# Two kernels fused at a double norm: one closed-form factor from both token sums in place of two factors taken in sequence

## The chip, the cores and the metric

The program runs on one core of one Trainium2 chip, in a single launch. The metric is the device time of the launch in microseconds (us), as the median of several executions. A second execution is taken with the hardware profiler; its records are the trace that is read here.

## The reference

Two transformer blocks run one behind the other on the same 256 tokens of width 1024, all in float32. Each block has two layers, each layer is feed-forward, mixer, feed-forward, and each of these begins with an RMS norm. The place of the change is the seam between the blocks, where two norms follow each other with nothing in between but the gains:

```python
EPS = 1e-6

def rmsnorm(x, g):
    xf = x.astype(jnp.float32)
    y = xf * lax.rsqrt(jnp.mean(xf * xf, axis=-1, keepdims=True) + EPS)
    return (y * g.astype(jnp.float32)).astype(x.dtype)
...
    return rmsnorm(x, final_norm)          # end of the first block
...
        h = modulate(rmsnorm_2(x, norm_g[l, 0]), mod[:, 0], mod[:, 1])   # start of the second, l = 0
        x = x + 0.5 * mod[:, 2][:, None, :] * swiglu_2(h, ffn_w1[l, 0], ffn_w2[l, 0])
```

With s1 the sum of x² over a token and s2 the sum of (g·x)², g being `final_norm`, the first factor is r1 = (s1/1024 + EPS)^-½, and the second norm sees the values r1·g·x, whose squares add up to r1²·s2. Its factor is r2 = (r1²·s2/1024 + EPS)^-½. The second block's feed-forward needs the product r1·r2 for its input, and r1 alone for the residual x.

## The kernel before

The activations are kept transposed: `x` is a tile of 128 partitions × 8 blocks × 256 tokens, the width being 8 × 128. Each matmul is made in fp32r parts: a value v is split in a rounded high part and the low rest, so that a weight chunk becomes `wh` (made on ACT at line 311) and `wl` (made on DVE at line 324, `wl = stg - wh`, in two halves of 128×1024), and the norm input becomes `Hh` and `Hl`. Weights stream from memory in chunks of 16 blocks through the staging tiles `stg`; the class `Stream` decides which chunk is prepared when. A scheduler puts the instructions of each engine in order when the program is built; each engine then runs its own list in order, with semaphores between engines.

A feed-forward (`ffn`, line 724) computes 22 output tiles; tile i takes 16 weight blocks. The norm's factor is not applied to its input. The first five tiles (`i < OLD`) multiply the gained but unnormed x (lines 614 to 616, three matmuls per block, `pp` in PSUM) and get the token's factor afterwards, as `t = pp * rs` on DVE at line 742, where `rs` holds the factor of each token in all 128 partitions. Meanwhile `renorm` (line 570) makes the normed input `H` block by block, which the tiles from the fifth on read (lines 598 and 599, two matmuls per block).

So the factor is made beside the first tiles, in three steps that sit in the middle of tile 1. After block 1 `norm_sum` runs. `token_sums` (line 518) has PE add up the squares over the partitions, two matmuls of one column each into a PSUM tile `pst`; `inv_root` (line 525) has DVE make the mean plus EPS (`ms`, line 529) and POOL raise it to the power -½ (`rcol`, line 531). After block 7 `norm_spread` has PE copy the factor of each token to all partitions (line 537, two transposes into `pbc`), and ACT copies that to `rs` (line 562).

All norms but one are single. The one at the seam, announced by `turn` (line 715) with `fin` set to the gain `final_norm`, has two accumulators of squares, `acc` and `acc2`, and takes two factors in sequence (lines 543 to 551). It spreads two of them: `rcol` is the product of both factors, for the feed-forward, and `r1` is the first one, by which `renorm` rescales x (line 588). In this text the stretch from the token sums to the spread is called the seam. Before it, on DVE, stand two products of the background work on the modulation (line 693), and after it the first `t`.

The helper tiles of the norm (`ms`, `rcol`, `q`, `q2`, `rc2`, `rs`) come from the pool `tp`, one place per tag and buffer. The pools of each stage (`act`, `H`, the mixers' tiles) are opened later and lie behind it in the on-chip memory.

Of the kernel before, what the change touches and what calls it, by code (L numbers as in the profile page):

```python
# [9 lines left out]
F32 = mybir.dt.float32  # L10
# [3 lines left out]
OP = mybir.AluOpType  # L14
# [3 lines left out]
P = 128  # L18
S = 256
D = 1024  # L20
# [5 lines left out]
EPS = 1e-6  # L26
# [344 lines left out]
class Kern:  # L371
# [166 lines left out]

    def norm_sum(self):
        nc, tp = self.nc, self.tp  # L540
        self.rcol = self.inv_root(self.token_sums(self.acc), D)
        if self.fin is not None:
            r1 = self.rcol
            q = tp.tile([P, 2], F32, name="q", tag="q")
            nc.vector.tensor_mul(q, r1[:, :2], r1[:, :2])
            q2 = tp.tile([P, 2], F32, name="q2", tag="q2")
            nc.vector.tensor_mul(q2, self.token_sums(self.acc2), q)
            r2 = self.inv_root(q2, D)
            self.rcol = tp.tile([P, 8], F32, name="rc2", tag="rc2")
            nc.vector.tensor_mul(self.rcol[:, :2], r1[:, :2], r2[:, :2])  # L550
            self.r1 = r1

    def norm_spread(self):
        self.rs = self.spread_rows(self.rcol)
# [1137 lines left out]
```

## Time and profile before

| | |
|---|---|
| median of 3 runs | 1996.35 us (1993.39 to 1996.38) |
| the profiled execution, its own time | 1991.56 us |
| span of its trace | 1989.8 us |
| PE busy | 1956.1 us (98%) |
| DVE busy | 1588.7 us (80%) |
| ACT busy | 1176.2 us (59%) |
| POOL busy | 188.9 us (9%) |
| granted TensorE clock, mean | 0.997 of full speed |

The span runs from the first to the last instruction that the profiler saw; 1.76 us of the execution's time lie around it. PE is TensorE's matmuls, DVE is VectorE, ACT is ScalarE and POOL is GpSimd. Matmuls are pipelined and their ends are modelled, so that the step from one matmul to the next is read from their starts. The seam lies at about 1011 to 1018 us of the span.

### The profile page before, as it was taken

Reading aid. Unit: us, or ns where it says so; the run is one execution under the profiler, and the core shown is the slowest. Engines: PE = TensorE matmul, PEld = TensorE weight load, DVE = VectorE, ACT = ScalarE, POOL = GpSimd, SP = SyncE. Lnnn points to the kernel's source line nnn. Section 1 sums busy time; section 2 is a strip of 40 time slices with the busy share of each in tenths; the row PEclk is TensorE's granted clock in tenths of the full one; section 3 lists DMA queues with packets and bytes.
Section 4 is the critical chain, followed back from the end, with each engine's and each line's share of the span. In section 5 each row is a group of like instructions: output and inputs, shape, how many; then the busy total and the mean of one; then the engine's idle time right before and its main releaser. Section 6 shows DMA issues by size and latency. Waiting matters only on the chain.

```text
span 1989.8 us, 33083 instructions
## 1 busy us (share of the span) xinstructions
PE 1956.1 (98%) x13146; PEld 1776.8 (89%) x13146; DVE 1588.7 (80%) x2572; ACT 1176.2 (59%) x1977; POOL 188.9 (9%) x207
## 2 busy tenths in 40 slices
PE   8999999999999999999999999999999999999998
PEld 8888989888988898988898889898899888889887
DVE  8986788987888788898789878898667666988663
ACT  6654566554555466655566546675546554877652
POOL 3001012000100101200110010120010001211001
PEclk9999999999999999999999999999999999999999
DMA  7976435887687643488758864368555556315551
GB/s 290 334 279 242 161 137 176 296 288 268 231 290 273 244 153 143 171 299 290 266 193 304 290 239 166 128 246 290 183 195 179 190 191 199 128 50 194 189 186 61
DMA packets 67868, 429.36 MB, mean 216 GB/s; under 512 B 11392, under 2 KB 14208, under 8 KB 16896
## 3 DMA queue, kind: packets, MB, share of 16 engines
q1 hardware_dynamic: 66992, 426.19, 59.6%
q8 instruction: 103, 1.69, 0.3%
q10 hardware_dynamic: 720, 1.05, 0.2%
q14 instruction: 53, 0.43, 0.1%
HBM read 426.16 MB, written 1.05 MB: 215 GB/s over the span
## 4 chain that ended last, share of the span: by engine, by line
PE 87%; DVE 8%; ACT 2%; issue 1%; DMA 1%; POOL 0%; SPq 0%; POOLq 0%; ACTq 0%; DVEq 0%
PE pp L598 25%; PE pd L598 16%; PE pp L599 13%; PE pd L599 8%; PE pp L614 5%; PE pp L615 5%; PE pp L616 5%; PE po L889 3%; DVE wl L324 3%; PE pt L1279 1%; ACT wh L311 0%; PE pav L1574 0%; POOL rcol L531 0%; PE pd L782 0%; DVE e L1068 0%
## 5 line engine op out<-in xcount | busy, mean ns | idle before, releaser
L324 DVE TENSOR_TENSOR wl<-stg,wh 128x1024 fp32r<-128x1024 f32 x642 | 779.7, 1241 | 122.0 <-PE pd L599 46.2
L311 ACT ACTIVATE wh<-stg 128x1024 fp32r<-128x1024 f32 x642 | 662.6, 1053 | 318.1 <-PE pp L598 106.8
L598 PE MATMUL pp<-H,wh 128*128 128x512 f32 x2176 | 754.8, 390 | 0.0
L599 PE MATMUL pp<-H,wl 128*128 128x256 f32 x2176 | 613.7, 282 | 0.0
L598 PEld LDWEIGHTS pp<-H,wh 128*128 128x128 f32 x2176 | 408.4, 188 | 85.1
L598 PE MATMUL pd<-act,wh 128*128 128x512 f32 x1386 | 480.8, 390 | 0.0
L599 PEld LDWEIGHTS pp<-H,wl 128*128 128x128 f32 x2176 | 412.1, 189 | 0.0
L599 PE MATMUL pd<-act,wl 128*128 128x256 f32 x1386 | 390.9, 282 | 0.0
L614 PE MATMUL pp<-Hh,wh 128*128 128x256 f32 (+1 forms) x1176 | 338.9, 288 | 6.8 <-ACT wh L282 6.4
L616 PE MATMUL pp<-Hh,wl 128*128 128x256 f32 (+1 forms) x1176 | 332.9, 283 | 0.6 <-DVE wl L324 0.6
L615 PE MATMUL pp<-Hl,wh 128*128 128x256 f32 x1176 | 332.7, 283 | 0.6 <-DVE Hl L679 0.6
L598 PEld LDWEIGHTS pd<-act,wh 128*128 128x128 f32 x1386 | 260.1, 188 | 54.4
L599 PEld LDWEIGHTS pd<-act,wl 128*128 128x128 f32 x1386 | 262.6, 189 | 0.0
L614 PEld LDWEIGHTS pp<-Hh,wh 128*128 128x128 f32 x1176 | 222.8, 189 | 10.8 <-ACT wh L282 6.4
L615 PEld LDWEIGHTS pp<-Hl,wh 128*128 128x128 f32 x1176 | 224.1, 191 | 1.7 <-DVE Hl L679 1.2
L616 PEld LDWEIGHTS pp<-Hh,wl 128*128 128x128 f32 x1176 | 223.6, 190 | 1.4 <-DVE wl L324 0.8
L693 DVE SCALAR_TENSOR_TENSOR stg<-stg,cond 128x1024 f32<-128x1024 f32 x144 | 176.3, 1226 | 29.2 <-DMA stg<-mw 27.0
L675 ACT ACTIVATE act<-a 128x256 fp32r<-128x256 f32 x176 | 73.4, 417 | 140.4 <-DVE a L751 127.8
L515 POOL TENSOR_TENSOR acc<-sq 128x256 f32<-128x256 f32 x16 | 17.8, 1116 | 1169.8 <-ACT sq L511 1169.7
L515 POOL TENSOR_TENSOR acc<-acc,sq 128x256 f32<-128x256 f32 x87 | 78.4, 904 | 337.7 <-ACT sq L511 336.8
L676 DVE TENSOR_TENSOR act<-a,act 128x256 fp32r<-128x256 f32 x176 | 75.3, 428 | 44.0 <-ACT act L675 44.0
L738 ACT ACTIVATE s<-t 128x256 f32<-128x256 f32 x136 | 56.6, 416 | 77.1 <-DVE t L607 76.9
(318 smaller groups left out, 2134.0 us busy)
## 6 DMA issues: line engine op xcount, KB each, us to landing
stg<-b SPq DMA_DIRECT2D x132, 1024.0 KB, 4.8
stg<-a SPq DMA_DIRECT2D x129, 1024.0 KB, 4.8
stg<-mw SPq DMA_DIRECT2D x72, 1024.0 KB, 5.4
stg<-m SPq DMA_DIRECT2D x32, 1024.0 KB, 4.8
stg<-m2a SPq DMA_DIRECT2D x14, 1024.0 KB, 4.9
stg<-m2b SPq DMA_DIRECT2D x12, 1024.0 KB, 4.7
stg<-nab SPq DMA_DIRECT2D x4, 1024.0 KB, 4.7
cond<-cond SPq DMA_DIRECT2D x6, 512.0 KB, 4.9
```

The lines of the kernel that those rows point to most:

```text
L311: self.k.nc.scalar.activation(h[:, sl], self.raw[c][:, sl], AF.Copy)
L324: self.k.nc.vector.tensor_sub(l[:, sl], t[:, sl], f(h[:, sl]))
L515: nc.gpsimd.tensor_tensor(s2, acc, sq, op=OP.add)
L598: mm(p, h, parts, start=start, stop=False)
L599: return mm(p[:, :S], l, parts[:, 1], start=False, stop=stop)
L614: mm(out[:, :n], h, self.Hh[:, kt, :n], start=start and clear, stop=False, skip_group_check=not clear)
L615: mm(out[:, :S], h, self.Hl[:, kt], start=False, stop=False, skip_group_check=not clear)
L616: return mm(out[:, :n], l, self.Hh[:, kt, :n], start=False, stop=stop, skip_group_check=not clear)
L675: nc.scalar.activation(hi, src, AF.Copy)
L676: nc.vector.tensor_sub(lo, src, f(hi))
L693: self.nc.vector.scalar_tensor_tensor(sl, sl, 1.0, self.cond, op0=OP.mult, op1=OP.mult, accum_out=self.mod[l][:, 2 * c + g:2 * c + g + 1])
L889: mm(p, w, x[:, kt], start=half + kt + n + i // 4 == 0, stop=half == 1 and kt == 3 and n == 2, skip_group_check=True)
```

## The change

The double norm no longer takes the second factor from the first one. Since r1² = 1/m with m = s1/1024 + EPS, the product of both factors has a closed form, r1·r2 = (s2/1024 + EPS·m)^-½. Both sums are taken first; DVE makes m (`ms`), s2/1024 (`q`) and EPS·m + q (`q2`), and POOL takes two powers that don't depend on each other, first that of `q2` (the product, `rcol`) and then that of `ms` (the first factor, `r1`). Three multiplications and one mean on DVE go, two other small operations come, and the tile `rc2` is gone.

```diff
     def norm_sum(self):
         nc, tp = self.nc, self.tp
-        self.rcol = self.inv_root(self.token_sums(self.acc), D)
-        if self.fin is not None:
-            r1 = self.rcol
-            q = tp.tile([P, 2], F32, name="q", tag="q")
-            nc.vector.tensor_mul(q, r1[:, :2], r1[:, :2])
-            q2 = tp.tile([P, 2], F32, name="q2", tag="q2")
-            nc.vector.tensor_mul(q2, self.token_sums(self.acc2), q)
-            r2 = self.inv_root(q2, D)
-            self.rcol = tp.tile([P, 8], F32, name="rc2", tag="rc2")
-            nc.vector.tensor_mul(self.rcol[:, :2], r1[:, :2], r2[:, :2])
-            self.r1 = r1
+        if self.fin is None:
+            self.rcol = self.inv_root(self.token_sums(self.acc), D)
+            return
+
+        p, p2 = self.token_sums(self.acc), self.token_sums(self.acc2)
+        m = tp.tile([P, 8], F32, name="ms", tag="ms")
+        nc.vector.tensor_scalar(m[:, :2], p, 1.0 / D, EPS, op0=OP.mult, op1=OP.add)
+        q = tp.tile([P, 2], F32, name="q", tag="q")
+        nc.vector.tensor_scalar(q, p2, 1.0 / D, None, op0=OP.mult)
+        q2 = tp.tile([P, 2], F32, name="q2", tag="q2")
+        nc.vector.scalar_tensor_tensor(q2, m[:, :2], EPS, q, op0=OP.mult, op1=OP.add)
+        self.rcol, self.r1 = [tp.tile([P, 8], F32, name="rcol", tag="rcol", bufs=4) for _ in range(2)]
+        for r, w in ((self.rcol, q2), (self.r1, m[:, :2])):
+            nc.gpsimd.tensor_tensor(r[:, :2], w, self.mhalf[:, :2], op=OP.pow)
```

The scheduler also orders the engines' lists anew around it. On DVE, in the kernel before, the seam runs from the first mean to the first `t`, with the two halves of one weight chunk's `wl` between:

```order
L529 TENSOR_SCALAR ms_10521<-pst_10518 128x2
L324 TENSOR_TENSOR wl_10631<-stg_10335,wh_10506 128x1024
L545 TENSOR_TENSOR q_10525<-rcol_10523 128x2
L324 TENSOR_TENSOR wl_10631<-stg_10335,wh_10506 128x1024
L547 TENSOR_TENSOR q2_10527<-pst_10528,q_10525 128x2
L529 TENSOR_SCALAR ms_10532<-q2_10527 128x2
L550 TENSOR_TENSOR rc2_10536<-rcol_10523,rcol_10534 128x2
L742 TENSOR_TENSOR t_10566<-pp_10452,rs_10559 128x512
```

In the changed kernel the same place on DVE reads:

```order
L547 TENSOR_SCALAR ms_10524<-pst_10518 128x2
L549 TENSOR_SCALAR q_10526<-pst_10521 128x2
L324 TENSOR_TENSOR wl_10627<-stg_10335,wh_10506 128x1024
L551 SCALAR_TENSOR_TENSOR q2_10528<-ms_10524,q_10526 128x2
L324 TENSOR_TENSOR wl_10627<-stg_10335,wh_10506 128x1024
L745 TENSOR_TENSOR t_10562<-pp_10452,rs_10555 128x512
```

None of the small operations waits for POOL any more, but `q2`, the input of the first power, stands behind the first half of `wl` and ahead of the second.

On PE, in the kernel before, the spread stands within a triple of matmuls of tile 1 (`pp_10503`), 28 matmuls behind the token sums:

```order
L616 MATMUL pp_10503<-Hh_72,wl_10393 128x258
L614 MATMUL pp_10503<-Hh_72,wh_10337 128x258
L537 MATMUL pbc_10556<-ident_75,rc2_10536 128x128 x2
L537 MATMUL pbc_10561<-ident_75,rcol_10523 128x128 x2
L615 MATMUL pp_10503<-Hl_73,wh_10337 128x256
```

In the changed kernel it stands 18 matmuls behind the sums:

```order
L619 MATMUL pp_10503<-Hh_72,wl_10393 128x258
L537 MATMUL pbc_10552<-ident_75,rcol_10530 128x128 x2
L537 MATMUL pbc_10557<-ident_75,rcol_10531 128x128 x2
L617 MATMUL pp_10503<-Hh_72,wh_10337 128x258
L618 MATMUL pp_10503<-Hl_73,wh_10337 128x256
```

The four transposes moved ten matmuls ahead, and both pairs still stand side by side; the second pair now reads the result of POOL's second power (`rcol_10531`).

Behind the seam DVE's list is reordered in places up to the end of this feed-forward. In the kernel before, the rows from the first `a` on are:

```order
L753 SCALAR_TENSOR_TENSOR a_10572<-t_10566,b_10568,s_10570 128x256
L742 TENSOR_TENSOR t_10619<-pp_10503,rs_10559 128x512
L685 TENSOR_REDUCE b_10621<-pp_10503 128x2
L324 TENSOR_TENSOR wl_10636<-stg_10388,wh_10628 128x1024
L676 TENSOR_TENSOR act_10451<-a_10572,act_10451 128x256
```

In the changed kernel:

```order
L756 SCALAR_TENSOR_TENSOR a_10568<-t_10562,b_10564,s_10566 128x256
L591 SCALAR_TENSOR_TENSOR x_70<-x_70,cols_74,rs_10560 128x256 x2
L580 TENSOR_TENSOR y_10669<-x_70,rs_10555 128x256
L679 TENSOR_TENSOR act_10451<-a_10568,act_10451 128x256
L679 TENSOR_TENSOR H_10572<-h_10575,H_10572 128x256
L679 TENSOR_TENSOR H_10572<-h_10593,H_10572 128x256
L745 TENSOR_TENSOR t_10615<-pp_10503,rs_10555 128x512
L688 TENSOR_REDUCE b_10617<-pp_10503 128x2
L324 TENSOR_TENSOR wl_10632<-stg_10388,wh_10624 128x1024
```

Two rescalings of x, one `y`, the first `act` and two parts of `H` moved ahead of the second `t` and of the next `wl`.

## Rows read from the trace of the kernel before

**Rows 1.** The page: busy time by engine, and the chain that ended last.
```profile
PE 1956.1 (98%) x13146; PEld 1776.8 (89%) x13146; DVE 1588.7 (80%) x2572; ACT 1176.2 (59%) x1977; POOL 188.9 (9%) x207
...
PE 87%; DVE 8%; ACT 2%; issue 1%; DMA 1%; POOL 0%; SPq 0%; POOLq 0%; ACTq 0%; DVEq 0%
```

**Rows 2.** PE's waits, 1010 to 1040 us: us in total, times, longest.
```profile
PE pbc L537 <- DVE rc L550: 1.7, 1, 1.7
```

**Rows 3.** Timeline at the seam, DVE and POOL: start us, length us.
```profile
1011.68 1.22 DVE L693 SCALAR_TENSOR_TENSOR stg<-stg,cond 128x1024 f32<-128x1024 f32 x1
...
1012.83 0.15 DVE L529 TENSOR_SCALAR ms<-pst 128x2 f32<-128x2 f32 x1
1012.90 1.21 DVE L324 TENSOR_TENSOR wl<-stg,wh 128x1024 fp32r<-128x1024 f32 x1
...
1013.06 1.62 POOL L531 TENSOR_TENSOR rcol<-ms,mhalf 128x2 f32<-128x2 f32 x1 [3.50 <-DVE ms L529]
...
1014.71 0.16 DVE L545 TENSOR_TENSOR q<-rcol 128x2 f32<-128x2 f32 x1 [0.60 <-POOL rcol L531]
...
1014.79 1.22 DVE L324 TENSOR_TENSOR wl<-stg,wh 128x1024 fp32r<-128x1024 f32 x1
...
1015.92 0.15 DVE L547 TENSOR_TENSOR q<-pst,q 128x2 f32<-128x2 f32 x1
1016.11 0.17 DVE L529 TENSOR_SCALAR ms<-q 128x2 f32<-128x2 f32 x1
1016.36 0.70 POOL L531 TENSOR_TENSOR rcol<-ms,mhalf 128x2 f32<-128x2 f32 x1 [1.68 <-DVE ms L529]
1017.09 0.16 DVE L550 TENSOR_TENSOR rc<-rcol 128x2 f32<-128x2 f32 x1 [0.81 <-POOL rcol L531]
```

**Rows 4.** Timeline at the seam, PE.
```profile
1014.24 0.28 PE L616 MATMUL pp<-Hh,wl 128*128 128x258 f32 x1
...
1015.42 0.28 PE L614 MATMUL pp<-Hh,wh 128*128 128x258 f32 x1
...
1017.40 0.40 PE L537 MATMUL pbc<-ident,rc 128*128 128x128 f32 x2 [1.69 <-DVE rc L550]
1017.64 0.38 PE L537 MATMUL pbc<-ident,rcol 128*128 128x128 f32 x2
...
1017.98 0.28 PE L616 MATMUL pp<-Hh,wl 128*128 128x258 f32 x1
```

**Rows 5.** POOL's powers elsewhere: their group (busy us, mean ns), two single ones.
```profile
L531 POOL TENSOR_TENSOR rcol<-ms,mhalf 128x2 f32<-128x2 f32 x16 | 22.3, 1395 | 50.1 <-DVE ms L529 46.7 <-DVE sp L419 3.4
...
202.33 1.22 DVE L324 TENSOR_TENSOR wl<-stg,wh 128x1024 fp32r<-128x1024 f32 x1
202.50 1.62 POOL L531 TENSOR_TENSOR rcol<-ms,mhalf 128x2 f32<-128x2 f32 x1 [3.43 <-DVE ms L529]
...
1981.74 0.71 POOL L531 TENSOR_TENSOR rcol<-ms,mhalf 128x2 f32<-128x2 f32 x1 [7.30 <-DVE ms L529]
...
1982.51 0.65 PE L537 MATMUL pbc<-ident,rcol 128*128 128x128 f32 x4 [1.04 <-POOL rcol L531]
```

**Rows 6.** Behind the seam: busy us by engine in a stretch; two rows of the timeline.
```profile
1018.00:1037.00 19.00, 19.00 (x161) 18.96 (x160) 18.75 (x41) 15.80 (x33) 3.54 (x4) 1.00 0.32 116
...
1032.91 0.69 DVE L742 TENSOR_TENSOR t<-pp,rs 128x512 f32<-128x512 f32 x1
...
1036.74 0.39 PE L598 MATMUL pp<-H,wh 128*128 128x512 f32 x1
```

**Rows 7.** One line's matmuls, ns min/median/max: `gh` of both layers, `Hh`; count of `H`.
```profile
L889 PE MATMUL po<-gh,wh x32: 277/280/282, 311.6 to 322.5; 128*128 128x256 f32 x32
...
L889 PE MATMUL po<-gh,wh x32: 276/276/280, 809.7 to 820.3; 128*128 128x256 f32 x32
...
L614 PE MATMUL pp<-Hh,wh x52: 280/283/288, 1018.1 to 1036.4; 128*128 128x258 f32 x52
...
L598 PE MATMUL pp<-H,wh 128*128 128x512 f32 x2176 | 754.8, 390 | 0.0
```

## The prediction

> **What bounds the kernel now.** The page comes first. PE is busy for 98% of the span and DVE for 80%, and the chain that ended last is 87% PE [rows 1]. So time is won or lost where PE stands still, and nearly nowhere else. The changed code runs for one norm out of all of them, once in 1989.8 us. PE's waits in the stretch around it are the second view: there is a single one, 1.69 us long, when the transposes wait for `rc2` [rows 2, 4]. That is the whole prize. The kernel before can lose 1.69 us here, 0.085% of the time, and no more.
>
> The timeline says what the 1.69 us are made of [rows 3]. The first mean `ms` starts at 1012.83, at once after the modulation's product on DVE. Half of a chunk's `wl` follows it on DVE at 1012.90, and POOL's first power runs from 1013.06 to 1014.68. DVE waits for it, makes `q`, is then taken by the second half of `wl`, and makes `q2` and the second mean only at 1015.92 and 1016.11. The second power runs from 1016.36 to 1017.06, DVE multiplies at 1017.09, and PE's first pair of transposes starts at 1017.40. PE had got there at 1015.71.
>
> **What the change does, part by part.** *Removed:* `q = r1²`, `q2`, the second mean and `rc2`, four small operations of 0.15 to 0.17 us each on DVE; *added:* `q` and `q2` in new form. I take the length of the new ones from those rows. Two fewer on DVE are 0.3 us of work, worth nothing by themselves, since DVE stands idle for 0.60 and 0.81 us in the seam anyway [rows 3]. If that idle time were gone, they would be worth 0.3 us of DVE and still not of PE. The token sums on PE are the same four matmuls at the same place; both sums must now be done before `q`, but PE did them together before, too.
>
> *Moved, on DVE:* the two powers' inputs. By DVE's new order `ms` stays at 1012.83, for the product ahead of it is the same. `q` comes 0.07 us later (the step from `ms` to `wl`, 1012.83 to 1012.90), at 1012.90, and the first half of `wl` at 1012.97. A half of `wl` holds DVE for 1.13 us (1014.79 to 1015.92), so `q2` starts at 1014.10 and the second half 0.08 us later (as from 1014.71 to 1014.79), at 1014.18, to end at 1015.39. So the product's power gets its input at 1014.10, where the old second mean came at 1016.11: 2.01 us earlier. Nothing on DVE waits for POOL any more.
>
> *Moved, on POOL:* the power of `q2` starts 0.23 us behind its input's start (1012.83 to 1013.06), at 1014.33. How long is it? The 16 powers of this shape last 22.3 us together and fall in two kinds. Twelve last 1.62 us or, once, 1.69; four last 0.70 or 0.71: 11 × 1.62 + 1.69 + 0.70 + 3 × 0.71 makes the 22.3 [rows 5]. All twelve long ones have a `wl` on DVE that began just ahead of them; beside the four short ones DVE does nothing. In both long ones shown the power ends 0.57 us after `wl` does: 1014.68 against 1014.11 [rows 3], and 204.12 against 203.55 [rows 5]. The short one of the seam is the old second power, which found DVE idle. In the new order the product's power has the second half of `wl` right beside it, begun 0.15 us earlier. So it is of the long kind and ends at 1015.39 + 0.57 = 1015.96.
>
> The Trainium skill speaks to this (GPSIMD Engine Reference, section Specifications): GpSimd's interfaces to SBUF are shared with VectorE, with contention when the VectorE instruction has two inputs in SBUF, as `wl` has. The rows agree, 1.62 against 0.70 us. By this rule the old sequence had one long power and one short one, and so has the new; a sum that took the bare 0.70 us for both would come out about 0.9 us better.
>
> *The second power* (of `ms`, the factor for x) stands behind the first on POOL. DVE is then idle, since its next row is `t`, which waits for `rs`. I take 0.70 us, the row nearest to it (the same operands, DVE idle): 1015.96 to 1016.66.
>
> The same skill (Perfetto Trace Analysis, section GPSIMD Engine Instruction) holds that a GpSimd span is unreliable and that the step between starts should be used. Here the reader of the old second power starts 0.73 us after the power did (1016.36 to 1017.09), so the trace supports the span; by the rule the step of two powers back to back could be less, which no row here shows, and a step near zero would make the sum below 0.4 us to the better side.
>
> *Moved, on PE:* the spread stands ten matmuls earlier. Ten matmuls take 1.18 us (1014.24 to 1015.42 [rows 4]), so PE gets to it at about 1014.5 in place of 1015.7. POOL's end reaches PE 0.06 us later (1982.45 to 1982.51 [rows 5]), so the first pair starts at 1016.02. The second pair stands right behind it and needs the second power: 1016.66 + 0.06 = 1016.72. In the kernel before this pair was never waited for; it had its factor since 1014.68. From the second pair's start to the second matmul behind it are 0.34 us (1017.64 to 1017.98), which makes 1017.06, and the ten matmuls that are now behind the spread bring PE to the matmul of 1017.98 at 1017.06 + 1.18 = 1018.24.
>
> **The sum.** 1018.24 − 1017.98 = 0.26 us later. The old chain of two powers with DVE between them is 2 us shorter up to the product's input; the long power (0.9 us), the second factor's power in front of PE (0.7 us) and the earlier place of the spread take all of that back. Against the profiled execution's own 1991.56 us this makes 1991.8; that execution lies 4.8 us under the median of the three runs, so I add the same 0.26 us to the median: 1996.35 + 0.26 = 1996.6 us.
>
> *Bounds of the unknown costs.* If the product's power were short (0.70), the powers would end at 1015.03 and 1015.73, and the sum is 1015.73 + 0.06 + 0.34 + 1.18 − 1017.98 = −0.67 us. If the second were long as well (1.62), it ends 0.92 us later, +1.18 us. Below everything lies −1.69 us, the wait gone altogether.
>
> *Behind the seam* PE does not wait again before 1040 [rows 2], though DVE is busy for 18.75 of 19 us there [rows 6]. `rs` comes 1.38 us earlier (first pair at 1016.02 in place of 1017.40), which gives DVE's new order that much more room, and PE, which doesn't wait, nothing.
>
> **The rivals.**
>
> *A gain in the seam.* The first power slips in ahead of the second half of `wl`, or the two overlap, and the time goes by −0.67 to −1.69 us, 1995.7 to 1994.7. For it: the new chain has fewer links. Against it: twelve of twelve powers that start beside a `wl` are long. It would be within 0.2% all the same.
>
> *DVE's new order makes PE wait behind the seam (slower).* Six rows of rescaling, `y`, `act` and `H`, all ahead of the second `t` now, could hold up DVE in a stretch where it has 0.25 us to spare. PE's tightest deadline that I find is tile 5, which reuses the PSUM of tile 3: DVE has read that by 1033.60 and PE gets there at 1036.74 [rows 6], a slack of 3.1 us. From a slip of 3.1 us on, each further one is PE's. Some 1.4 us of head start must be lost first. The price of a slip that a trace could show as time, say twice the slack, is 6.2 − 3.1 = 3.1 us, and 4.3 us with the seam's upper bound of 1.2: 2000.6. Against it: the work is the same, only its order changes, and four of the six rows (`y`, `act`, `H`) make what PE needs by tile 5 or later anyway.
>
> *Where tiles lie.* The tag `rc2`, two buffers of 32 bytes, is gone from `tp`, so all the stages' tiles move by 64 bytes. The trace has one case of a move: `gh` in the second layer's mixer lies 32 bytes off from the first layer's in the built program, and its matmuls last 276 ns and not 280 [rows 7]. Were 64 bytes to do as much to the 4,352 matmuls that read `H` (2 × 2,176 [rows 7]), that would be 4 ns × 4,352 = 17 us, 1979 or 2014. Against it: `Hh` has 272 columns of 4 bytes, so every other block of it is off by 64 bytes in this very way, and its 52 matmuls stay within 280 to 288 ns around 283; what 32 bytes do, a second 32 seem to undo.
>
> *The change doesn't do what it says.* The two powers are independent, but POOL runs them one by one and PE reads both in one place. In that sense it is already my forecast.
>
> **How the numbers follow.** About what a measurement can tell here from no change is 0.2%, 4 us. The forecast, a loss of 0 to 1.2 us in the seam, has 0.80; the gain in the seam 0.07. DVE's order making PE wait: 0.03. The place of tiles: 0.05, shared by both signs, of which 0.01 would stay under 0.2%. The rest, 0.05, is a drift of medians, for single executions differ by as much as 0.24% (1991.56 to 1996.38): 0.03 downward, since the median lies near the upper end, and 0.02 upward. So same has 0.80 + 0.07 + 0.01 = 0.88, faster 0.02 + 0.03 and slower 0.03 + 0.02 + 0.02, rounded from below and above to 0.055 and 0.065. The range takes the bounds (1994.7 to 1997.5) and widens them by what the runs differ, more downward, where two of four executions lie, than upward: 1992.5 to 1999.0.
>
> **What would show it right or wrong.** Right: `ms` and `q` ahead of `wl` at about 1012.9, `q2` between its halves, a first power of 1.6 us and a second of 0.7 back to back, PE waiting about 1.5 us for the first pair and some 0.3 us more within the spread, and the matmul of 1017.98 at the same time to within half a microsecond. Wrong in the seam: a first power of 0.7 us. Wrong as a whole: a wait of PE for DVE or ACT between 1018 and 1050, or another length of the matmuls that read `H` and `act` over the whole span.

## The result, and the profile after

| | us |
|---|---|
| changed kernel, median of 4 runs | 2014.23 (2010.03 to 2016.05) |
| kernel before, median of 4 runs | 1996.09 (1993.39 to 1996.38) |
| ratio, with its 95% interval | 1.0096 [1.0084, 1.0107] |
| changed kernel, profiled execution, its span and mean clock | 2014.67, 2012.9, 0.994 |

The change makes the kernel 18.1 us slower. That is outside the range of the prediction, and it is the time of one of its rivals, "where tiles lie" (2014), which had a chance of 0.05 for both signs together.

The page of the changed kernel answers to [rows 1]. First the busy times, then the chain, then the costliest groups on PE (busy us, mean ns | idle us before):

```profile
PE 1979.4 (98%) x13146; PEld 1778.1 (88%) x13146; DVE 1591.1 (79%) x2570; ACT 1176.4 (58%) x1977; POOL 190.3 (9%) x207
...
PE 87%; DVE 8%; ACT 2%; issue 1%; DMA 1%; POOL 0%; POOLq 0%; SPq 0%; ACTq 0%; DVEq 0%
...
L601 PE MATMUL pp<-H,wh 128*128 128x512 f32 x2176 | 765.6, 396 | 0.0
...
L601 PEld LDWEIGHTS pp<-H,wh 128*128 128x128 f32 x2176 | 408.5, 188 | 98.3
L601 PE MATMUL pd<-act,wh 128*128 128x512 f32 x1386 | 487.7, 396 | 0.0
...
L601 PEld LDWEIGHTS pd<-act,wh 128*128 128x128 f32 x1386 | 260.2, 188 | 62.9
```

PE has 23.3 us more to do, and waits no longer than before. The matmuls of 512 columns, the same in number, last 396 ns and not 390 ([rows 7], and the first row below); the prediction had named another length of these matmuls as a sign of being wrong as a whole. These lengths are modelled, so a second sign is worth more: the weight loads ahead of them stand idle for 98.3 + 62.9 = 161.2 us. The same two rows of the kernel before say 139.5, so that 21.7 us are found there:

```profile
L598 PE MATMUL pd<-act,wh 128*128 128x512 f32 x1386 | 480.8, 390 | 0.0
...
L598 PEld LDWEIGHTS pp<-H,wh 128*128 128x128 f32 x2176 | 408.4, 188 | 85.1
...
L598 PEld LDWEIGHTS pd<-act,wh 128*128 128x128 f32 x1386 | 260.1, 188 | 54.4
```

Starts are measured, and say it best. In a feed-forward each weight block takes a pair of matmuls, 512 columns with `wh` and 256 with `wl`. The timeline of PE in the second feed-forward of the changed kernel (start us, length us):

```profile
400.12 0.40 PE L601 MATMUL pp<-H,wh 128*128 128x512 f32 x1
...
400.48 0.39 PE L601 MATMUL pp<-H,wh 128*128 128x512 f32 x1
...
400.83 0.40 PE L601 MATMUL pp<-H,wh 128*128 128x512 f32 x1
...
401.19 0.39 PE L601 MATMUL pp<-H,wh 128*128 128x512 f32 x1
401.42 0.28 PE L602 MATMUL pp<-H,wl 128*128 128x256 f32 x1
401.53 0.40 PE L601 MATMUL pp<-H,wh 128*128 128x512 f32 x1
```

The pairs alternate: by the trace's full figures one step is 346 ns and the next 361. In the kernel before nearly every step lies between 345 and 348 ns, with a mean of 346.7. The same is read from the view of one line in a stretch (count, lengths min/median/max, first and last start). First the kernel before, then the changed kernel in its second and in its third feed-forward:

```profile
L598 PE MATMUL pp<-H,wh x174: 389/390/391, 379.9 to 439.9; 128*128 128x512 f32 x174
```

```profile
L601 PE MATMUL pp<-H,wh x171: 392/402/402, 379.6 to 439.7; 128*128 128x512 f32 x171
...
L601 PE MATMUL pp<-H,wh x203: 392/392/392, 559.9 to 629.9; 128*128 128x512 f32 x102
```

60.0 us over 173 steps are 346.8 ns. In the changed kernel it is 60.1 us over 170 steps, 353.5 ns, in the second feed-forward, and 70.0 over 202, 346.5, in the third. So the loss is not everywhere. By the mean over all starts of each feed-forward, six of the eight take 353.3 ns from their first pair to their last, and two take 346.7. A feed-forward has 272 such pairs with `H` and 176 with `act` ([rows 7]: 2,176 is 8 × 272), and 448 × 6.67 ns are 2.99 us; the last one has 154 with `act`, which makes the 1,386 of the page. Six times 2.99 us, less these 22 pairs, is 17.8 us. The rest of the 23.1 us between the two spans is the clock: 2012.9 × (1 − 0.994) is 12.1 us of lost clock, 1989.8 × (1 − 0.997) is 6.0. The sum, 17.8 + 6.1 = 23.9, meets the 23.1 within the rounding of the clock. Two more traces of the kernel before (e16 and e17 below) have a mean clock of 0.995, so this second part differs from one execution to the next without any change.

The seam itself, the answer to [rows 3], comes 9.05 us late before any changed code has run (`ms` at 1021.88, before at 1012.83). The long steps of the first two feed-forwards make 6.0 us of that; besides, the granted clock is 0.50 from 274.3 to 281.1 us in this trace, where the kernel before has 1.00. Timeline of DVE, POOL and PE there:

```profile
1021.88 0.15 DVE L547 TENSOR_SCALAR ms<-pst 128x2 f32<-128x2 f32 x1
...
1021.95 0.15 DVE L549 TENSOR_SCALAR q<-pst 128x2 f32<-128x2 f32 x1
...
1022.02 1.22 DVE L324 TENSOR_TENSOR wl<-stg,wh 128x1024 fp32r<-128x1024 f32 x1
...
1023.15 0.16 DVE L551 SCALAR_TENSOR_TENSOR q<-ms,q 128x2 f32<-128x2 f32 x1
1023.22 1.22 DVE L324 TENSOR_TENSOR wl<-stg,wh 128x1024 fp32r<-128x1024 f32 x1
1023.38 1.62 POOL L554 TENSOR_TENSOR rcol<-q,mhalf 128x2 f32<-128x2 f32 x1 [5.18 <-DVE q L551]
1024.98 0.69 POOL L554 TENSOR_TENSOR rcol<-ms,mhalf 128x2 f32<-128x2 f32 x1
...
1025.06 0.52 PE L537 MATMUL pbc<-ident,rcol 128*128 128x128 f32 x2 [1.89 <-POOL rcol L554]
...
1025.73 0.69 PE L537 MATMUL pbc<-ident,rcol 128*128 128x128 f32 x2 [0.15 <-POOL rcol L554]
```

The order and the two powers, 1.62 and 0.69 us back to back, are as forecast, and PE waits for 1.89 + 0.15 us in place of the 1.69 of [rows 2, 4]. One thing that the sum did not have follows: PE's granted clock is halved behind this wait, as the view by stretches shows (us, PE busy (count), granted clock, DMA share, GB/s):

```profile
1022.00:1025.00 3.00, 1.17 (x10) 1.00 0.61 197
1025.00:1026.00 1.00, 0.79 (x4) 0.64 1.08 459
1026.00:1028.00 2.00, 2.00 (x11) 0.50 1.01 418
1028.00:1030.00 2.00, 2.00 (x16) 0.83 0.29 123
```

### The profile page after: what moved, and what is told of

Read it like the earlier page. It is cut to its first block, busy times and chain, and to the rows that moved or that the text cites. A ratio compares the mean times of both kernels' runs of the same rounds, so it can differ in the third digit from the quotient of the medians.

```text
span 2012.9 us, 33083 instructions
## 1 busy us (share of the span) xinstructions
PE 1979.4 (98%) x13146; PEld 1778.1 (88%) x13146; DVE 1591.1 (79%) x2570; ACT 1176.4 (58%) x1977; POOL 190.3 (9%) x207
## 3 DMA queue, kind: packets, MB, share of 16 engines
q8 instruction: 103, 1.69, 0.3%
## 4 chain that ended last, share of the span: by engine, by line
PE 87%; DVE 8%; ACT 2%; issue 1%; DMA 1%; POOL 0%; POOLq 0%; SPq 0%; ACTq 0%; DVEq 0%
PE pp L601 25%; PE pd L601 16%; PE pp L602 13%; PE pd L602 8%; PE pp L617 5%; PE pp L618 5%; PE pp L619 5%; PE po L892 3%; DVE wl L324 3%; PE pt L1282 1%; PE pav L1577 0%; ACT wh L311 0%; PE pd L785 0%; PE pv L667 0%; DVE e L1071 0%
## 5 line engine op out<-in xcount | busy, mean ns | idle before, releaser
L601 PE MATMUL pp<-H,wh 128*128 128x512 f32 x2176 | 765.6, 396 | 0.0
L601 PEld LDWEIGHTS pp<-H,wh 128*128 128x128 f32 x2176 | 408.5, 188 | 98.3
L601 PE MATMUL pd<-act,wh 128*128 128x512 f32 x1386 | 487.7, 396 | 0.0
L601 PEld LDWEIGHTS pd<-act,wh 128*128 128x128 f32 x1386 | 260.2, 188 | 62.9
```

Source lines behind the costliest of these rows:

```text
L601: mm(p, h, parts, start=start, stop=False)
```

## The experiments

**The theory.** The tag `rc2` took 64 bytes of the pool `tp`. With it gone, `act` and `H`, the moving operands of the pairs, start 64 bytes lower in the built program: 96 bytes behind a multiple of 128, and not 32. The weights `wh` and `wl` start on a multiple of 128 in both kernels. This place makes PE's steps longer. **The rival:** the new order of the instructions, in the seam and on DVE behind it, costs the time.

All runs but the last four are told together in this table; the places are bytes behind the start of the weights modulo 128, read from the built programs, and a step is the mean distance from one pair's start to the next over whole feed-forwards of the profiled execution, without the single steps of over 0.37 us in which PE paused (at most six in a feed-forward). All kernels but the two marked have the changed kernel's instructions in its order.

| run | `act` / `H` from `wh` | from `wl` | step, ns | median us | ratio to before |
|---|---|---|---|---|---|
| before (order of before) | 32 | 32 | 346.7 in all 8 | 1996.09 | |
| changed | 96 | 96 | 353.3 in 6 of 8 | 2014.23 | 1.0096 |
| e1_gap64 | 32 | 32 | 346.7 in all 8 | 1994.15 | 1.0002 [0.9993, 1.0012] |
| e2_no_rc2 (order of before) | 96 | 96 | 353.3 in 6 of 8 | 2011.37 | 1.0090 [1.0075, 1.0105] |
| e3_off0 | 0 | 0 | 353.3 in 2 of 8 | 2000.56 | 1.0036 [1.0024, 1.0048] |
| e5_off64 | 64 | 64 | 353.3 in all 8 | 2016.09 | 1.0113 [1.0098, 1.0129] |
| e6_off32 | 32 | 32 | 346.7 in all 8 | 1994.24 | 1.0001 [0.9991, 1.0010] |
| e7_act_only | 96 / 32 | 96 / 32 | `act` 353.3, `H` 346.7 | 2003.65 | 1.0046 [1.0029, 1.0063] |
| e8_rel32 | 32 | 32 | 346.7 in all 8 | 1994.06 | 1.0003 [0.9994, 1.0013] |
| e9_rel96 | 96 | 96 | 353.3 in 7 of 8 | 2012.55 | 1.0089 [1.0070, 1.0109] |
| e10_wl64 | 32 | 96 | 348.9 in 7, 353.3 in 1 | 2003.43 | 1.0050 [1.0033, 1.0068] |
| e11_wh64_wl0 | 96 | 32 | 350.0 in 6, two others | 2004.74 | 1.0057 [1.0041, 1.0073] |
| e12_112_16, one run | 112 / 16 | 112 / 16 | `act` 353.1, `H` 346.7 in 7, 359.9 in 1 | 2007.17 | |
| e13_48_80, one run | 48 / 80 | 48 / 80 | `act` 350.0, `H` 353.3 | 2010.45 | |

The kernel before, run beside them, had medians of 1994.15 (e1 to e5), 1994.33 (e6 to e9) and 1993.29 (e10 to e13).

**The change without the move, the move without the change.** The first puts 64 unused bytes where `rc2` was; the second is the kernel before with `rc2` put into a tag that is there anyway.

```diff
 e1_gap64 (changed kernel, end of norm_sum)
+        tp.tile([P, 16], F32, name="gap", tag="gap", bufs=1)
 e2_no_rc2 (kernel before)
-            self.rcol = tp.tile([P, 8], F32, name="rc2", tag="rc2")
+            self.rcol = tp.tile([P, 8], F32, name="rc2", tag="rcol", bufs=4)
```

> The changed kernel with one unused tile of 64 bytes in the place of the vanished rc2: every later tile stands again where it stood before, and the instructions and their order are those of the change. Theory of places: the 128x512 matmuls fall back from 396 to 390 ns and the time is 1996.6 us (before + 0.26 us from the seam, 1995 to 1998). Rival, the new order or the seam costs it: 2014 us, and 396 ns stay. Rival, something of the chip in the run after: neither is fixed.

> The kernel before, with rc2 put into one of the four rcol buffers: same instructions in the same order, both factors in sequence, but all later tiles stand 64 bytes lower. Theory of places: 396 ns for the 128x512 matmuls and 2014 us, without any change of the norm. Rival, order or seam: 1996 us and 390 ns.

The changed kernel with the filler is as fast as the kernel before, 1994.15 us each. The kernel before without `rc2` loses 17.2 us. The view of the line in one stretch, of the first and then of the second:

```profile
L602 PE MATMUL pp<-H,wh x189: 390/390/390, 1059.7 to 1124.9; 128*128 128x512 f32 x189
```

```profile
L598 PE MATMUL pp<-H,wh x199: 392/402/402, 1059.8 to 1129.8; 128*128 128x512 f32 x199
```

These are steps of 65.2/188 = 346.8 ns and 70.0/198 = 353.5. So the whole loss goes with the place, and the rival falls: the new order costs nothing that can be measured.

**Other places.** A filler of 32 bytes (e3), one buffer of `q` less (e5), one of `q` and of `q2` less (e6).

```diff
 e3_off0
+        tp.tile([P, 8], F32, name="gap", tag="gap", bufs=1)
 e5_off64, e6_off32 (e6 the second line too)
-        q = tp.tile([P, 2], F32, name="q", tag="q")
+        q = tp.tile([P, 2], F32, name="q", tag="q", bufs=1)
-        q2 = tp.tile([P, 2], F32, name="q2", tag="q2")
+        q2 = tp.tile([P, 2], F32, name="q2", tag="q2", bufs=1)
```

> The changed kernel with 32 unused bytes in place of rc2: H and act start at a multiple of 128 bytes (before: 32 past one, after: 96 past one). If the offset within 128 bytes decides, a length of its own: the gh rows of after give 282 ns at 0 and at 96 against 280 at 32 and 276 at 64, so I expect 394 to 396 ns and about 2012 us. If only the step of 64 bytes from the old place mattered, half of it: 393 ns, 2005 us. Rival, order or seam: 2014 us.

> The changed kernel with one buffer in place of two for q: all later tiles another 32 bytes lower, H and act at 64 past a multiple of 128. By the offset within 128 bytes this is the place where gh was fastest (276 ns against 280 at 32): 384 to 388 ns for the 128x512 matmuls and 1975 to 1990 us, faster than the kernel before. If the length only grows with the distance from the old place (96 bytes now): 399 ns and 2023 us. Rival, order or seam: 2014 us.

> The changed kernel with one buffer for q and one for q2: all later tiles stand 128 bytes below those of before, H and act again 32 past a multiple of 128. If the offset within 128 bytes decides: 390 ns for the 128x512 matmuls and the time of before, 1994 us (1992 to 1998). If the absolute place or the distance moved decides, or the period is longer than 128: anything from 393 to 400 ns, 2001 to 2025 us.

I had taken the length to fall evenly with the place, and 64 to be the best. e3 came out at 2000.56 us and not at 2012, and 64 is the worst, with the long step in every feed-forward (3,562 pairs × 6.67 ns = 23.8 us by the steps, 21.9 by the medians). 128 bytes lower is as good as the kernel before, which fits a place that counts modulo 128. A stretch of e5, 70.0 us over 198 steps, 353.5 ns:

```profile
L601 PE MATMUL pp<-H,wh x199: 397/397/398, 1059.8 to 1129.8; 128*128 128x512 f32 x199
```

**One operand alone.** 64 unused bytes between `act` and `H`.

```diff
 e7_act_only
             act = ap.tile([P, NF, 2, S], F32R, name="act")
+            ap.tile([P, 16], F32, name="gap")
```

> The changed kernel with 64 unused bytes between act and H: act stays 96 past a multiple of 128, H (and the feed-forward's smaller tiles behind it) stand at 32 again. If each moving operand's own place decides: 396 ns for the 1386 matmuls that read act, 390 for the 2176 that read H; the time is 1386 x 6 ns = 8.3 us over before, 2002.5 us. If one of the two tiles alone is at fault, 1994 or 2013 us.

Each operand pays for its own place: 1,386 pairs × 6.67 ns are 9.2 us, and 9.3 were measured. The stretch of `act` with the long step, then one of `H`:

```profile
L601 PE MATMUL pd<-act,wh x129: 392/402/402, 959.7 to 1004.9; 128*128 128x512 f32 x129
...
L601 PE MATMUL pp<-H,wh x174: 390/390/390, 874.9 to 934.9; 128*128 128x512 f32 x174
```

**The place of what?** Now the weights move too, by 64 unused bytes ahead of `wh`. In e8 `act` and `H` stand 96 bytes behind a multiple of 128, the slow place, and the weights 64. In e9 `act` and `H` are back at the very place of the kernel before, and the weights stand at 64.

```diff
 e8_rel32, e9_rel96 (e8 with one buffer of q and q2 each, as e6)
         self.hp = ctx.enter_context(tc.tile_pool(name="hp", bufs=Stream.AHEAD + 1))
+        self.hp.tile([P, 16], F32, name="gap", tag="gap", bufs=1)
```

> The changed kernel with wh and wl (and the norm's tiles between) 64 bytes higher and q, q2 in one buffer each, so that act and H stay where the change put them, 96 past a multiple of 128, and the weights stand at 64 in place of 0. If the place relative to the weights decides (96 - 64 = 32, as before): 390 ns and 1994 us. If the moving operand's own offset decides: 396 ns and 2012 us.

> The changed kernel with wh and wl 64 bytes higher and everything behind them with them: act and H stand exactly where they stood in the kernel before, at 32, the weights at 64 in place of 0. If the moving operand's own offset decides: 390 ns and 1994 us. If the place relative to the weights decides (32 - 64 = 96 modulo 128, as in the changed kernel): 396 ns and 2012 us.

e8 first, then e9:

```profile
L602 PE MATMUL pp<-H,wh x203: 391/392/392, 1059.8 to 1129.8; 128*128 128x512 f32 x102
```

```profile
L602 PE MATMUL pp<-H,wh x199: 392/392/402, 1059.9 to 1129.9; 128*128 128x512 f32 x199
```

The old place of `act` and `H` is slow once the weights have moved away (353.5 ns a step), and their slow place is fast once the weights have followed (346.5). So what counts is the distance between the moving operand and the weights; the weights were moved by 64 bytes alone.

**Which weights?** e10 has the 64 bytes between `wh` and `wl`, e11 ahead of both and between them.

```diff
 e10_wl64 (in split_hi, behind the tile of wh; e11 a second one ahead of wh)
+            k.hp.tile([P, 16], F32, name="gap", tag="gap", bufs=1)
```

> The changed kernel with 64 unused bytes between the tiles of wh and wl, so that wl and all that lies behind it move by 64 bytes: act and H start 32 bytes behind a multiple of 128 (as in the kernel before), wh on the multiple, wl 64 behind it. So the moving tiles lie 32 bytes from wh's place and 96 from wl's. Theory: the load of the weights that come next runs beside the matmul, and beside the 512 columns of H with wh it is wl that is loaded; so wl's place would count, and the time would be about 2012 us with a mean of 396 ns for the 512-column matmuls. Rival: the place relative to the weights that are multiplied (wh) counts: 390 to 392 ns, 1994 us for those matmuls, and the 256-column ones with wl might be longer instead.

> The mirror image: 64 unused bytes ahead of wh and 64 more between wh and wl, with q and q2 at one buffer each, so that act and H start 32 bytes behind a multiple of 128, wh 64 behind it, and wl on it. The moving tiles lie 96 bytes from wh's place and 32 from wl's. If wl's place counts (the load beside the long matmul): about 1994 us, 390 to 392 ns. If wh's place counts: about 2012 us, 396 ns. If both count in part, both this run and its mirror image lie between 1994 and 2012.

Neither alone decides. Both runs lie half way, 10.1 and 11.5 us above the kernel before, with steps of their own between the other two. The second feed-forward of e10, 60.0 us over 172 steps (348.8 ns), and of e11, 60.2 over 172 (350.0):

```profile
L602 PE MATMUL pp<-H,wh x173: 389/393/397, 379.6 to 439.6; 128*128 128x512 f32 x173
```

```profile
L603 PE MATMUL pp<-H,wh x173: 393/393/394, 379.7 to 439.9; 128*128 128x512 f32 x173
```

**Finer places.** `act` and `H` shifted by 16 bytes within their tiles, for a place faster than 32.

```diff
 e12_112_16, e13_48_80 (e13 with one buffer of q and q2 each; act in the same way)
+        self.H = pool.tile([P, KD * 2 * S + 8], F32R, name="H")[:, 4:4 + KD * 2 * S].rearrange("p (n h s) -> p n h s", n=KD, h=2)
```

> The changed kernel with act and H moved by 16 bytes within their tiles: act starts 112 bytes and H 16 bytes behind a multiple of 128, the weights on it. A look at the means alone. If the mean falls off evenly around 32 bytes, H (16) lies between the values of 0 and 32, 391 to 392 ns, and act (112) between those of 96 and 0, 394 to 397 ns. If places have a grain of 32 bytes, H reads as at 0 (393) and act as at 96 (396 to 397). A mean below 389 ns for one of them would be a faster place than the one of the kernel before.

> As the one before, with q and q2 at one buffer each: act starts 48 bytes and H 80 bytes behind a multiple of 128, the weights on it. If the mean falls off evenly around 32 bytes, act (48) lies between the values of 32 and 64, 392 to 394 ns, and H (80) between those of 64 and 96, 396 to 397. If places have a grain of 32 bytes, act reads as at 32 (390 to 392) and H as at 64 (397). A mean below 389 ns would be a faster place.

No step is below 346.7 ns. `H` at 16 has that in seven feed-forwards and 359.9 in the eighth, though its mean length of 389 ns looks best of all: starts decide, not modelled lengths. None of the places tried is faster than that of the kernel before.

**Program or execution?** The same program has feed-forwards with either step. Two more traces of the changed kernel and two of the kernel before, unaltered:

> The changed kernel, unaltered, for a second trace of it. In the first one the step from one pair of matmuls (512 columns with wh, 256 with wl) to the next was 353.3 ns from the first pair to the last in the first, second, fifth, sixth, seventh and eighth feed-forward, and 346.7 ns, as in the kernel before, throughout the third and fourth. If the program decides which feed-forward takes the long step (addresses, order), the same six have it again. If the place only makes the long step possible and the execution decides, the set is another one, of 4 to 8 feed-forwards, and the time is about 1994 us and 3.0 us (448 pairs by 6.67 ns) for each.

> The same once more, a third trace of the changed kernel: the same six feed-forwards with the long step if the program decides, another set if the execution does. At the seam the granted clock was halved for 3.4 us behind PE's wait in the first trace; if that belongs to the change it shows in most traces of this seam (it did in 4 of 12 so far), if to chance it comes and goes.

> The kernel before, unaltered, for a second trace: every pair of every feed-forward at 346.7 ns if its place leaves no longer step, at some 1992 to 1997 us. At the seam no halved clock if that belongs to the change; a stretch of 3.4 us at half clock there would show that the old seam can have it too.

> The kernel before once more, a third trace: again 346.7 ns throughout, 1992 to 1997 us, and the granted clock at the seam looked at as in the run ahead of it.

| step of `H` by feed-forward, ns | 1 | 2 | 3 | 4 | 5 to 8 | us |
|---|---|---|---|---|---|---|
| changed, first trace | 353.3 | 353.3 | 346.7 | 346.7 | 353.3 | 2014.67 |
| e14_after_again | 353.3 | 346.7 | 353.3 | 346.7 | 353.3 | 2011.97 |
| e15_after_again2 | 348.2, mixed | 346.7 | 353.3 | 353.3 | 353.3 | 2014.22 |
| both of the kernel before | 346.7 | 346.7 | 346.7 | 346.7 | 346.7 | 1993.48, 1994.00 |

The second and the third feed-forward of the second trace, to be held against those of the first above:

```profile
L601 PE MATMUL pp<-H,wh x174: 392/392/392, 379.9 to 439.8; 128*128 128x512 f32 x174
...
L601 PE MATMUL pp<-H,wh x199: 392/392/402, 559.9 to 629.8; 128*128 128x512 f32 x199
```

They have changed places. The sets of e14 and e15 differ as well. So among the first four the execution decides it, and at this distance the place only makes the long step possible; the last four are long in all three traces.

The mixed feed-forward of e15 shows when a step can change. PE pauses in it at 111.6 us, for two steps of 444 and 454 ns; up to there 51.3 us over 148 steps are 346.6 ns, and from there 21.2 over 60 are 353.3:

```profile
L601 PE MATMUL pp<-H,wh x149: 392/392/392, 59.9 to 111.2; 128*128 128x512 f32 x149
...
L601 PE MATMUL pp<-H,wh x61: 392/392/402, 112.5 to 133.7; 128*128 128x512 f32 x61
```

In e11 the third feed-forward changes its step three times, each time at such a pause (561.6, 567.4 and 641.7 us). Within a run of pairs of one operand without a pause no step changes in any of the 18 traces.

## Why the prediction was wrong

**The step that failed** is the weighing of the rival "where tiles lie". The prediction named the cause, its unit (64 bytes) and its time (2014), and put it at 0.05 (0.02 of it for slower) by one argument: "what 32 bytes do, a second 32 seem to undo". That came from `Hh`, whose blocks lie 64 bytes apart in turn and whose matmuls all last the same. But `Hh` is read in triples of 256 and 258 columns, which take another rhythm than the pairs of 512 and 256, and the pairs are what PE does for most of its time. No row of the kernel before shows the pairs at a second place. Its pairs all stand at one, which e3 to e13 show to be as good as any tried; so a move could only lose or do nothing, and the price, up to 3,562 pairs by some ns, was far above every term of the sum. The size was nearly right by accident: 4 ns × 4,352 = 17 us for `H`; measured were 6.67 ns a pair, for `act` as well, in six feed-forwards of eight. So the sum had the removal of the tile `rc2` at nothing, and it cost 18 us (e1, e2).

**The seam** was right, part by part. e1, with the place restored, shows it without the 9 us of delay:

```profile
1016.12 0.15 DVE L547 TENSOR_SCALAR ms<-pst 128x2 f32<-128x2 f32 x1
...
1017.63 1.62 POOL L554 TENSOR_TENSOR rcol<-q,mhalf 128x2 f32<-128x2 f32 x1 [5.11 <-DVE q L551]
1019.23 0.69 POOL L554 TENSOR_TENSOR rcol<-ms,mhalf 128x2 f32<-128x2 f32 x1
...
1019.31 0.43 PE L537 MATMUL pbc<-ident,rcol 128*128 128x128 f32 x2 [1.83 <-POOL rcol L554]
...
1019.98 0.43 PE L537 MATMUL pbc<-ident,rcol 128*128 128x128 f32 x2 [0.24 <-POOL rcol L554]
...
1021.57 0.28 PE L620 MATMUL pp<-Hh,wl 128*128 128x258 f32 x1
```

This `ms` is 3.29 us later than in [rows 3]. Taken off, the first pair of transposes starts at 1016.02 (forecast 1016.02), the second at 1016.69 (1016.72), and the last row, which is the matmul of 1017.98 in [rows 4], at 1018.28 (1018.24). The loss is 0.30 us, where 0.26 was forecast, and it is no accident of e1: from the start of `ms` to this matmul it takes 5.15 us in all four traces of the old seam and 5.42 to 5.45 in ten of the new one (the other four have a halved clock there, of which below). PE came to the spread at 1014.19 and not at 1014.5, so that it waited 1.83 us where 1.5 were forecast. The long power beside `wl` and the short one behind it are there in all 14 traces of the new seam; the gain in the seam did not come. DVE's new order makes PE wait nowhere behind the seam up to 1045 in e1.

**Missing from the sum** was the halved clock behind the wait. From the last token sum to the 45th matmul behind it (the transposes not counted), the old seam takes 7.56 to 7.85 us in four traces (before, e2, e16, e17; mean 7.73). The new one takes 7.46 to 8.40 in ten traces without a halved clock (mean 7.77), and 9.49 to 9.78 in the four that have it (the changed kernel's first, e6, e8, e9). That is 1.9 us in 4 of 14 against 0 of 4. PE stands still about as long in both seams, so this can be chance; whether it belongs to the change stays open. In the medians it isn't seen, for e6 and e8, which have it in the profiled execution, are at 1.0001 and 1.0003.

## What to carry to other kernels

Removing a small helper tile moves every tile that is opened behind it: compare the start addresses of the large matmul operands in the two built programs, modulo 128 and relative to the weights, before an edit is costed at nothing. Where they moved, put back the place with a filler of the same size, and only then judge the edit; 64 unused bytes took back all 18 us here. Judge it by the step between starts in each stage, since a mean of modelled lengths shows 6 ns of 390 where six stages of eight lose 2% and two nothing.

## What the runs showed of the hardware

A run of matmul pairs settles into one mean step and keeps it as long as PE does not pause: 346.7, 348.9, 350.0, 353.3 (353.1 for `act` in e12) or, once, 359.9 ns, and whole feed-forwards took one of these, but for one each of e11 and e15, which changed at pauses. Which of them is seen depends on the distance, modulo 128 bytes, of the moving operand from the weights; at one distance it can differ from one execution to the next (96), or from one feed-forward to another (0). Only at a distance of 32 bytes was it 346.7 in all eight feed-forwards, in each of six traces; at 64 it was 353.3 in all eight of one trace. The same mean is made up in several ways: at 96 steps of 346 and 361 ns alternate, at 0 (e3) two of 349 or 350 are followed by one of 361, at 64 all are 353 or 354.

The other engines' traffic is not needed to keep the long step. In the changed kernel's first trace 70 pairs of `H` had neither DVE nor ACT at work beside them, and 49 of them still took the long 360 or 361 ns. DMA transfers ran beside each of the 70, so that no row leaves those out. The Trainium skill (SBUF — State Buffer, section "SBUF: two separate sides") says that among the engines only the port pair shared by VectorE and GpSimd causes contention, and that PE never waits on another engine for its reads. These 70 pairs agree, as far as DVE and ACT go. That PE's own two reads, the moving operand and the next weights, get into each other's way would fit e8 to e11, but it was only argued: no run separates them, and how the lock comes about stays open.
